# A hybrid encoder layer in float32: causal mask added on VectorE, and the feed-forward net's first gate weights in buffers of the output projection's last block

## Chip, cores and metric

The kernel runs on one core of one Trainium2 chip. The metric is the device time of one execution in microseconds (us), the median over runs. The engines are TensorE (PE, with its weight loads PEld), VectorE (DVE), ScalarE (ACT), GpSimd (POOL) and SyncE (SP), whose queue issues all DMAs here.

## Reference

One layer of a streaming encoder on x of 1024 tokens by 1024 channels, float32. Cut to what matters:

```
proj = x @ w_in                                   # q, k, v of attention; q, f, i, g of the recurrence; two gates
y_a  = fox_attention(q_a, k_a, v_a, log_f)        # 8 heads of 64: softmax(q k^T/8 + F[t] - F[s], causal) v, F = cumsum(log f)
y_b  = hgrn2(...)                                 # 4 heads of 128, gated linear recurrence, RMS norm, gate
merged = sigmoid(gate_a) * (y_a @ w_pa) + sigmoid(gate_b) * (y_b @ w_pb)
x = layer_norm(2**.25 * x + merged @ w_o, ln1_g, ln1_b)
u, g = split(x @ w_ff_in)                         # 2816 hidden channels each
x = layer_norm(2**.25 * x + (silu(g) * u) @ w_ff_out, ln2_g, ln2_b)
```

## The kernel before

**Arithmetic.** Nearly every product is three matmuls of 128x512: each operand is split into a rounded high part (a copy on ACT) and the low rest (a subtraction on DVE), and high x high, high x low and low x high are summed in PSUM (`split`, L336; `mm3`, L365). Large products go by Strassen-Winograd: seven quarter products p1 to p7 with sums of quarter operands, made on DVE (names t1 to t4, s1 to s4).

**Stages.** v projections; forget gates; the first q and k projection (`qk_first`, L624); eight attention heads in four pairs (`attention`, L667), with the next pair's q and k projection (`qk_project`); four recurrence heads (`hgrn`) with their projections; gate projections (`gate`, `GatePair`); branch projections and merge; output projection with layer norm, eight token tiles t = 0 to 7 (L1191); the feed-forward net's first product in 22 chunks of 128 hidden channels (`Chunk`, L1275; the first two chunks run together, L1352 to L1402, the others by `chunk`, L1322); its second product with the last layer norm.

**What sets the order.** Every call on an engine goes into a list (`Plan.add`, L89). `Plan.schedule` (L160) simulates the five queues with fixed costs, takes the call that could start first, and writes the calls out in that order (`issue`, L268). So each engine's order is fixed at build time, each engine works it off strictly in order, and any call that is added or moved can reorder others. All calls carry the line L279 in the profile, so instructions are told apart by the names of their tiles. Equal ready times are decided by rank; `plan.early` (L65) lowers the rank of what is built under it. Buffers come from tagged pools (L294), given in the order of first use, except for the tags in `LOOSE`; a tile waits until the one before it in its buffer is no longer used.

**Attention.** For each head the kernel loads the head's negative forget sums into two rows of `box1` by a broadcast DMA (L675), and POOL adds the causal mask to a copy for the diagonal blocks, in two halves of 128x512 (L678). DVE then adds scores and these sums and takes the maximum in one instruction (profile: CUSTOM_DVE, tiles `p<-s,box`), ACT takes the exponential with the row sum (`soft` is the small tile of maximum, sum and reciprocal), POOL divides by the row sum, and TensorE transposes (`pt`) and multiplies by the values (`pv`). In the first pair's projection TensorE's product p7 goes into the bank `qk_pt`, out of which DVE must first have read the sum u2 (`qk_u`).

**Output projection.** Its weights lie in split form, per half hf and contraction block c: c = 0, 1 in an "x" buffer (`wox`), 2, 3 in the small wh and wl buffers, 4, 5 in "kb", 6, 7 in "pf" (L1162 to L1170). A tile t takes 48 matmuls, c = 0 to 7 for hf = 0, then for hf = 1; then come residual, statistics (`lnst`), layer norm, eight transposes (`x1t`) and the splits of the net's operands (X11, X12 for t < 4, X22 and S1 to S4 for t > 3; `xs` in the profile).

**The net's entry.** The weights of chunks 0 and 1, gate and up, four blocks of 512 KB, lie in one "x" buffer (`raws`, L1353), which is the one that `wox` gives up. Products p1 and p2 of both chunks (banks `fa`, operands X11 and X12, weights `Tp1`, `Tp2`) need only gate weights and the first four token tiles; p5 and p4 (banks `fc`, `fd`) need sums with the up weights and all eight tiles.

```
    plan.early = EARLY
    raws = take("x", [4, KC, P], "w01_r")
    ks = [Chunk(c, (raws[:, 2 * c], raws[:, 2 * c + 1])) for c in range(2)]
    banks = [[next_bank(f"f{n}{c}") for n in "abcd"] for c in range(2)]
```

Of the kernel before, what the change touches and what calls it, by code (L numbers as in the profile page):

```python
# [11 lines left out]
AF = mybir.ActivationFunctionType  # L12
# [4 lines left out]
P = 128  # L17
S = 1024
D = 1024
KC = D // P  # L20
NT = S // P
HA, DH = 8, 64
HB = 4
NB = 512
# [7 lines left out]
EARLY = 3000  # L32
# [250 lines left out]
def trunk(ctx: ExitStack, tc, a: dict, out: bass.AP):  # L283
    nc = tc.nc
    plan = Plan(tc)
    sync, act, dve, pool, pe = (plan.queue(n, e) for n, e in (
        ("SP", nc.sync), ("ACT", nc.scalar), ("DVE", nc.vector), ("POOL", nc.gpsimd), ("PE", nc.tensor)))
# [17 lines left out]
    def take(tag, shape, name, dt=F32):  # L305
        return plan.tile(root, [P] + shape, dt, tag, name, BUFS[tag])
# [4 lines left out]
    def half(tag, name, dt=F32):  # L311
        return take(tag, [NB], name, dt)
# [4 lines left out]
    def keep(shape, name, dt=F32):  # L317
        return plan.tile(cst, shape, dt, "k_" + name, name, 1)
# [46 lines left out]
    def mm3(o, lh, ll, rh, rl, first, last, more={}):  # L365
        mm(o, lh, rh, start=first, stop=False, **more)
        mm(o, lh, rl, start=False, stop=False, **more)
        mm(o, ll, rh, start=False, stop=last, **more)
# [48 lines left out]
    def load(b, cs=range(4)):  # L417
        tiles, src = b
        for c in cs:
            sync.dma_start(tiles[c // 2][:, c % 2, :], src[c])  # L420
# [21 lines left out]
    for k, b, A, p, o in ((0, b11, A11, "p1", vx), (1, b21, A12, "p2", vy)):  # L442
        T = stationary4("v" + p)
        raw = rows(b)
# [130 lines left out]
    causal = const("causal", [P, 2, P], BF16, "mask")  # L575
# [91 lines left out]
    def attention(p, qk):  # L667
        q2, k2, kl = qk
        for i in range(2):
# [5 lines left out]
            sync.dma_start(box1[:, r, :], nf_d[h].partition_broadcast(P))  # L675
            for hf in range(2):
                plain, masked = (nfx[:, b0 + 4 * hf:b0 + 4 * hf + 4].rearrange("p (j c) t -> p j c t", c=2) for b0 in (0, NT))
                pool.tensor_add(masked, plain, causal[:, None].to_broadcast([P, 2, 2, P]))  # L678
            vhl = take("hl", [NT, 2, DH], f"vhl{h}", F32R)
            vsrc = va[:, :, h * DH:(h + 1) * DH]  # L680
            split(vhl[:, :, 0, :], vhl[:, :, 1, :], vsrc)
# [1 line left out]
            for qb in range(NT):  # L683
                n = (qb + 1) * P
# [35 lines left out]
                g = qb // 4  # L720
# [20 lines left out]
    raw = half("gt", "once_r")  # L741
# [305 lines left out]
    for n in range(PLAIN + 4, 2 * KC, 2):  # L1047
        k = GatePair(n)
# [33 lines left out]
    for i, src in enumerate((ya_d, yb_d)):  # L1082
        yh, yl = [], []
        for c in range(4):
            raw = raw_load(src[c], [S], f"yr{i}{c}")
# [30 lines left out]
        s_ = blk(t % 4)  # L1116
        return mh[t // 4][:, c, s_], ml[t // 4][:, c, s_]

    lnst = take("gt", [NT, 2, 6], "lnst")

    def lnrow(gname, bname):
        res = []
# [7 lines left out]
    def stats(t, hf):  # L1130
        dve.bn_stats(lnst[:, t, hf, :], z[t][:, hs(hf)])

    def layer_norm(t, gb, st=None, out=None):
        norm = small([P, 4], "norm")
        mv, ve, rstd = norm[:, :2], norm[:, 2:3], norm[:, 3:]
        dve.bn_aggr(mv, (lnst[:, t] if st is None else st).rearrange("p a b -> p (a b)"))
        dve.tensor_scalar(ve, mv[:, 1:2], LN_EPS, None, op0=ALU.add)
        pool.tensor_tensor(rstd, ve, mhalf[:, :1], op=ALU.pow)
        for hf in range(2):
            zt = z[t][:, hs(hf)]  # L1140
            dve.scalar_tensor_tensor(zt, zt, mv[:, 0:1], gb[0][hf], op0=ALU.subtract, op1=ALU.mult)
        for hf in range(2):
            zt = z[t][:, hs(hf)]
            dve.scalar_tensor_tensor(zt, zt, rstd, gb[1][hf], op0=ALU.mult, op1=ALU.add)
            if out is not None:
                sync.dma_start(out[:, hs(hf)], zt)
# [3 lines left out]
    wo = {}  # L1150
# [20 lines left out]
    OTAGS = ("s", "s", "s", "h", "h", "pv")  # L1171
    accs = [[bank(OTAGS[(2 * t + hf) % 6], f"o{hf}_{t}") for hf in range(2)] for t in range(NT)]

    def wo_mm(t, hf, c):
        lh, ll = mtok(t, c)
        mm3(accs[t][hf], lh, ll, *wo[hf, c], c == 0, c == KC - 1)

# [11 lines left out]
    for t in range(NT):  # L1191
        if t == 0:
            for c in range(KC):
                for i in range(3):
                    for hf in range(2):
                        wo_mm(i, hf, c)
        elif t > 2:
            for hf in range(2):
                for c in range(KC):
                    wo_mm(t, hf, c)  # L1200
        for hf in range(2):
            zt = z[t][:, hs(hf)]
            dve.scalar_tensor_tensor(zt, zt, ALPHA, accs[t][hf], op0=ALU.mult, op1=ALU.add)
            stats(t, hf)
        layer_norm(t, gb1)
        s_ = blk(t % 4)
        tps = []
        for g in range(2):
            tp = bank("pt", f"x1t{t}_{g}")
            for c in range(4):  # L1210
                tr(tp[:, blk(c)], z[t][:, blk(4 * g + c)], ident)
            if t < 4:
                h, l = (X11, X12)[g]
                split(h[:, :, s_], l[:, :, s_], by4(tp))
            tps.append(by4(tp))
        if t < 4:
            continue
        if t == 4:
            X22, S1 = operand("x", "x22"), operand("x", "xs1")
            r2s = [take(f"wr{i}", [2, NB], f"r2s{i}") for i in range(2)]  # L1220
        r1, r2 = (by4(x) for x in (half(("ph", "tt")[t % 2], f"r1_{t}"), r2s[t // 2 - 2][:, t % 2, :]))
        act.copy(r1, tps[0])
        split(X22[0][:, :, s_], X22[1][:, :, s_], tps[1])
        act.copy(r2, tps[1])

        def first_sums(s_=s_, r1=r1, r2=r2, t=t):
            s1 = by4(half("gt", f"s1r{t}"))
            dve.tensor_add(s1, r1, r2)
            split(S1[0][:, :, s_], S1[1][:, :, s_], s1)

        def next_sums(s_=s_, r1=r1, r2=r2):
            dve.tensor_sub(r1, f(X11[0])[:, :, s_], r1)
            dve.tensor_add(r1, r1, f(X11[1])[:, :, s_])
            dve.tensor_sub(r2, r2, r1)

        late.append((s_, r1, r2))
        if t < NT - 1:
            first_sums()
            next_sums()
# [9 lines left out]
    def next_bank(name):  # L1249
        n = turns["bank"]  # L1250
        turns["bank"] += 1
        return bank(BANKS8[n % 8], name)
# [22 lines left out]
    class Chunk:  # L1275
        def __init__(self, c, raw=None):
            self.c = c
            self.g, self.u = raw or (take("pf", [KC, P], f"w{n}{c}_r") for n in "gu")
            for i, t in enumerate((self.u, self.g)):
                sync.dma_start(t, a["w_ff"][c, i])  # L1280
            self.r = {}

        def sums(self, *names):
            g, u = self.g, self.u
# [64 lines left out]


    first_sums()
    plan.early = EARLY  # L1352
    raws = take("x", [4, KC, P], "w01_r")  # L1353
    ks = [Chunk(c, (raws[:, 2 * c], raws[:, 2 * c + 1])) for c in range(2)]
    banks = [[next_bank(f"f{n}{c}") for n in "abcd"] for c in range(2)]
    for k, o in zip(ks, banks):
        mul(k, "p1", o[0], True, True)
        k.p1 = half("ph", f"p1_{k.c}")
        act.copy(k.p1, o[0])
    for k, o in zip(ks, banks):  # L1360
        mul(k, "p2", o[0], False, True)
        k.sl = half("gt", f"sl{k.c}")
        act.activation(k.sl, o[0], AF.Silu)
    plan.early = 0
    OPS["p5"] = S1
    for k, o in zip(ks, banks):
        k.sums("1", "2")
# [69 lines left out]
    u = [half(("wh0", "wl0", "wh1", "wl1")[i], f"fu{i}") for i in range(4)]  # L1437
    ai = {"p1": 0, "p5": 1, "p6": 2, "p7": 3, "p4": 4, "p2": 5, "p3": 6}
    gb2 = lnrow("ln2_g", "ln2_b")
    lnst = take("gt", [NT, 2, 6], "lnst2")  # L1440
    XS = ("x",) * 5
    for prod in ("p1", "p5", "p6", "p4", "p7", "p2"):
        if prod == "p7":
# [2 lines left out]
        for g in range(len(GR)):  # L1446
            d, n = group(prod, ai[prod], g)
# [149 lines left out]
```

## Time and profile before

| | |
|---|---|
| Median of 3 runs | 1478.47 us (1478.4 to 1479.2) |
| Profiled execution | 1477.74 us, of which the span is 1475.8 us |
| TensorE busy | 1451.7 us, 98% of the span |
| VectorE, ScalarE, GpSimd busy | 75%, 45%, 7% |
| DMA | 172.84 MB, mean 117 GB/s |
| Mean granted TensorE clock | 0.996 of full speed |

The profile is one execution, taken by the hardware profiler. A row "PE fa <- ACT Tp_0h: 4.0, 1, 4.0" in the view of waits says that TensorE, before an instruction on tile fa, was idle 4.0 us in total, once, until ACT had written Tp_0h. A row of the timeline has start, duration, engine, line, operation, output <- inputs, shape and count, and in brackets the idle time ahead of it with what ended it; buffer numbers are left out. Windows give each engine's busy time (and number of instructions) in a stretch and the mean granted clock. A matmul's duration overlaps the next one's; what counts is the distance of starts.

### The profile page before, as it was taken

What the parts mean: (1) busy time and instruction counts of PE and PEld (TensorE: products, weight loads), DVE (VectorE), ACT (ScalarE), POOL (GpSimd) and SP (SyncE); (2) the same over time, 40 slices, a digit from 0 to 9 for tenths busy, and PEclk for the clock granted to TensorE, in tenths of its full rate; (3) what the DMA queues carried; (4) which work ended last, traced back from release to release, by engine and by line L of the source; (5) the groups of instructions that cost most, each with busy time, mean ns of one, the idle gap of its engine ahead of it and who ended that gap; (6) DMA issues with size and microseconds to landing.
All of it is one profiled execution on the core that took longest, in us unless ns stands there. A gap on an engine that the chain in (4) does not pass through costs nothing.

```text
span 1475.8 us, 19031 instructions
## 1 busy us (share of the span) xinstructions
PE 1451.7 (98%) x6807; PEld 1190.5 (81%) x6807; DVE 1109.4 (75%) x2088; ACT 669.3 (45%) x1157; POOL 97.7 (7%) x116
## 2 busy tenths in 40 slices
PE   9999999999999999999999899999999999999998
PEld 6777878888888887788888788888888888888886
DVE  7987686676797799744848897676666666798597
ACT  6536677577466465334611443332333333434430
POOL 0012142230000001000001000000000000000000
PEclk9999999999999999999999999999999999999999
DMA  7122112111111135347710304332332335976741
GB/s 263 31 87 75 48 54 79 42 51 36 58 59 50 58 122 178 134 145 242 246 47 1 114 32 143 103 94 94 96 101 103 107 107 182 350 268 218 248 159 58
DMA packets 70287, 172.84 MB, mean 117 GB/s; under 512 B 7968, under 2 KB 8864, under 8 KB 70192
## 3 DMA queue, kind: packets, MB, share of 16 engines
q1 hardware_dynamic: 70192, 171.62, 34.9%
q8 instruction: 54, 0.88, 0.3%
q14 instruction: 41, 0.34, 0.1%
HBM read 134.57 MB, written 37.03 MB: 116 GB/s over the span
## 4 chain that ended last, share of the span: by engine, by line
PE 89%; DVE 5%; DMA 2%; ACT 2%; issue 1%; POOL 0%; SPq 0%; DVEq 0%; ACTq 0%; POOLq 0%
PE p L279 14%; PE fb L279 11%; PE fc L279 8%; PE bps L279 8%; PE fa L279 8%; PE pps L279 6%; PE o L279 6%; PE gps L279 5%; PE gs L279 5%; PE vx L279 3%; PE s L279 2%; PE pv L279 2%; PE kps L279 2%; PE pt L279 2%; PE qps L279 2%; PE vy L279 1%
## 5 line engine op out<-in xcount | busy, mean ns | idle before, releaser
L279 PE MATMUL p<-dp 128*128 128x512 f32 (+1 forms) x957 | 210.0, 382 | 0.0
L279 PEld LDWEIGHTS p<-dp 128*128 128x128 f32 x957 | 175.3, 188 | 34.8
L279 PE MATMUL fc<-xs,Tp 128*128 128x512 f32 x528 | 126.9, 389 | 0.0
L279 PE MATMUL fb<-xs,Tp 128*128 128x512 f32 x528 | 126.7, 389 | 0.0
L279 PE MATMUL fa<-x,Tp 128*128 128x512 f32 x480 | 115.7, 389 | 0.5 <-DVE u L279 0.5
L279 PEld LDWEIGHTS fc<-xs,Tp 128*128 128x128 f32 x528 | 99.0, 188 | 20.7 <-ACT xs L279 0.2
L279 PEld LDWEIGHTS fb<-xs,Tp 128*128 128x128 f32 x528 | 99.1, 188 | 20.6
L279 ACT CAST Tp<-t 128x512 fp32r<-128x512 f32 x88 | 54.5, 620 | 118.1 <-PE fc L279 71.1
L279 DVE TENSOR_TENSOR Tp<-t,Tp 128x512 fp32r<-128x512 f32 x88 | 60.7, 691 | 60.3 <-ACT Tp L279 59.9
L279 PEld LDWEIGHTS fa<-x,Tp 128*128 128x128 f32 x480 | 90.0, 188 | 19.5 <-ACT p L279 0.9
L279 ACT CAST dp<-dap 128x1024 fp32r<-128x1024 f32 (+1 forms) x42 | 41.2, 982 | 99.7 <-PE p L279 43.4
L279 PE MATMUL bps<-xh,wb_l 128*128 128x512 f32 x192 | 76.5, 399 | 0.2
L279 PE MATMUL bps<-xh,wb_h 128*128 128x512 f32 x192 | 75.7, 395 | 0.4 <-ACT hbg L279 0.4
L279 PE MATMUL bps<-xl,wb_h 128*128 128x512 f32 x192 | 75.8, 395 | 0.0
L279 POOL TENSOR_TENSOR norm<-norm,mhalf 128x1 f32<-128x1 f32 x16 | 14.6, 913 | 881.2 <-DVE norm L279 881.2
L279 DVE TENSOR_TENSOR tl<-pt,th 128x512 fp32r<-128x512 f32 (+1 forms) x96 | 50.5, 552 | 18.7 <-ACT th L279 18.1
L279 DVE TENSOR_TENSOR dp<-dap,dp 128x1024 fp32r<-128x1024 f32 (+1 forms) x42 | 47.4, 1132 | 20.1 <-ACT dp L279 20.1
L279 POOL TENSOR_SCALAR p<-p,soft 128x384 f32<-128x384 f32 (+4 forms) x64 | 48.6, 767 | 164.3 <-DVE soft L279 128.6
L279 ACT ACTIVATE p<-p,soft 128x384 f32<-128x384 f32 (+4 forms) x64 | 49.5, 774 | 20.4 <-DVE soft L279 20.0
L279 PE MATMUL fb<-x,Tp 128*128 128x512 f32 x240 | 57.7, 389 | 0.0
L279 ACT CAST th<-pt 128x512 fp32r<-128x512 f32 (+1 forms) x96 | 43.0, 478 | 25.2 <-PE pt L279 23.6
L279 PE MATMUL gps<-xh,wg_h 128*128 128x512 f32 x128 | 52.2, 408 | 1.1 <-ACT wg_h L279 1.1
(511 smaller groups left out, 3490.0 us busy)
## 6 DMA issues: line engine op xcount, KB each, us to landing
dbp<-in_w_fo SPq DMA_DIRECT2D x45, 512.0 KB, 4.7
dap<-a_d SPq DMA_DIRECT2D x35, 512.0 KB, 4.8
a_d<-ar SPq DMA_DIRECT2D x42, 256.0 KB, 3.5
wu_r<-in_w_ff SPq DMA_DIRECT2D x20, 512.0 KB, 3.9
wg_r<-in_w_ff SPq DMA_DIRECT2D x20, 512.0 KB, 3.7
a_d<-as SPq DMA_DIRECT2D x33, 256.0 KB, 2.5
wg_r<-in_w_g SPq DMA_DIRECT2D x16, 512.0 KB, 4.4
sg<-gate_d SPq DMA_DIRECT2D x32, 256.0 KB, 3.7
```

The source lines that it names most:

```text
L279: getattr(q.engine, method)(*args, **kw)
```

## The change

It does two things. The causal mask is added by DVE and not by POOL. And the net's entry is laid out anew:

- The gate weights of chunks 0 and 1 go into two "pf" buffers of their own, and p1's results into a third; only the up weights go into the "x" buffer. The gates are loaded first, the ups only after p1 and p2 are written down. `plan.early` is no longer used there.
- The output projection's last tile starts with c = 6, 7 of both halves, so that it is done with the "pf" buffers first.
- Chunk 1's four banks are taken in another order (its `fa` gets the bank tag pv and not pt).
- The statistics tile `lnst` has a buffer of its own and is used by the second layer norm too; a Silu of one element at t = 1 loads ACT's table ahead.
- A later chunk loads gate before up (`Chunk.load`: names "gu").

```
-                pool.tensor_add(masked, plain, causal[:, None].to_broadcast([P, 2, 2, P]))
+                dve.tensor_add(masked, plain, causal[:, None].to_broadcast([P, 2, 2, P]))
...
-    lnst = take("gt", [NT, 2, 6], "lnst")
+    lnst = keep([P, NT, 2, 6], "lnst")
+    warm = keep([P, 1], "warm")
...
-    def wo_mm(t, hf, c):
+    def wo_mm(t, hf, c, first=0, last=KC - 1):
         lh, ll = mtok(t, c)
-        mm3(accs[t][hf], lh, ll, *wo[hf, c], c == 0, c == KC - 1)
+        mm3(accs[t][hf], lh, ll, *wo[hf, c], c == first, c == last)
...
-            for hf in range(2):
-                for c in range(KC):
-                    wo_mm(t, hf, c)
+            ahead = (6, 7) if t == NT - 1 else ()
+            cs = ahead + tuple(c for c in range(KC) if c not in ahead)
+            for hf, c in [(hf, c) for part in (cs[:len(ahead)], cs[len(ahead):]) for hf in range(2) for c in part]:
+                wo_mm(t, hf, c, cs[0], cs[-1])
...
+        if t == 1:
+            act.activation(warm, lnst[:, t, 1, :1], AF.Silu)
...
-            for i, t in enumerate((self.u, self.g)):
-                sync.dma_start(t, a["w_ff"][c, i])
             self.r = {}
+            if not raw:
+                self.load("gu")
+
+        def load(self, names):
+            for n in names:
+                sync.dma_start(getattr(self, n), a["w_ff"][self.c, "ug".index(n)])
...
-    plan.early = EARLY
-    raws = take("x", [4, KC, P], "w01_r")
-    ks = [Chunk(c, (raws[:, 2 * c], raws[:, 2 * c + 1])) for c in range(2)]
-    banks = [[next_bank(f"f{n}{c}") for n in "abcd"] for c in range(2)]
+    graws = [take("pf", [KC, P], f"wg{c}_r") for c in range(2)]
+    uraws = take("x", [2, KC, P], "wu01_r")
+    p1s = take("pf", [2, NB], "p1s")
+    ks = [Chunk(c, (graws[c], uraws[:, c])) for c in range(2)]
+    for k in ks:
+        k.load("g")
+    banks = [[next_bank(f"f{n}{c}") for n in ("abcd", "dabc")[c]] for c in range(2)]
+    banks[1] = banks[1][1:] + banks[1][:1]
...
-        k.p1 = half("ph", f"p1_{k.c}")
+        k.p1 = p1s[:, k.c]
...
-    plan.early = 0
+    for k in ks:
+        k.load("u")
...
-    lnst = take("gt", [NT, 2, 6], "lnst2")
```

The planner then writes other orders. At the first attention head, DVE's order before (Tqkp4l, Tqkp7l are low weight parts of products p4 and p7, vhl1 the second head's values, qk0_u2 the sum u2):

```order
L279 TENSOR_TENSOR wq0_r_188<-wq0_r_188,wqk_t2_190 128x512
L279 TENSOR_TENSOR vhl0_217<-va_107,vhl0_217 128x8x64
L279 TENSOR_TENSOR Tqkp4l_216<-wq0_r_188,Tqkp4h_215 128x512
L279 TENSOR_TENSOR Tqkp7l_214<-wq0_r_188,Tqkp7h_213 128x512
L279 SCALAR_TENSOR_TENSOR q2_0_0_197<-qk0_s_194,q2_0_0_197 64x512
L279 TENSOR_TENSOR vhl1_286<-va_107,vhl1_286 128x8x64
L279 SCALAR_TENSOR_TENSOR q2_0_1_198<-qk0_s_194,q2_0_1_198 64x512
L279 TENSOR_TENSOR qk0_u2_192<-qk0_pt_195,qk0_p1_191 128x512
L279 TENSOR_TENSOR qk0_u2_192<-qk0_s_196,qk0_u2_192 128x512
```

DVE's order there now (box1 <- box1, causal is a mask add; wq1 are the next pair's q weights):

```order
L279 TENSOR_TENSOR wq0_r_188<-wq0_r_188,wqk_t2_190 128x512
L279 TENSOR_TENSOR vhl0_217<-va_107,vhl0_217 128x8x64
L279 TENSOR_TENSOR box1_104<-box1_104,causal_163 128x512
L279 TENSOR_TENSOR Tqkp4l_216<-wq0_r_188,Tqkp4h_215 128x512
L279 TENSOR_TENSOR Tqkp7l_214<-wq0_r_188,Tqkp7h_213 128x512
L279 SCALAR_TENSOR_TENSOR q2_0_0_197<-qk0_s_194,q2_0_0_197 64x512
L279 TENSOR_TENSOR box1_104<-box1_104,causal_163 128x512 x2
L279 SCALAR_TENSOR_TENSOR q2_0_1_198<-qk0_s_194,q2_0_1_198 64x512
L279 TENSOR_TENSOR qk0_u2_192<-qk0_pt_195,qk0_p1_191 128x512
L279 TENSOR_TENSOR box1_104<-box1_104,causal_163 128x512
L279 TENSOR_TENSOR qk0_u2_192<-qk0_s_196,qk0_u2_192 128x512
L279 TENSOR_TENSOR vhl1_286<-va_107,vhl1_286 128x8x64
```

Three mask adds stand ahead of the first half of u2 and one between its halves; vhl1 is put behind.

SP's order of loads at the net's entry before (wu and wg are a chunk's up and gate weights, w01 the four blocks of chunks 0 and 1):

```order
L279 DMA wo1_3_r_1486<-in_w_o 128x1024
L279 DMA wu2_r_1594<-in_w_ff 128x1024
L279 DMA wg2_r_1593<-in_w_ff 128x1024
L279 DMA w01_r_1542<-in_w_ff 128x1024 x4
L279 DMA wu3_r_1616<-in_w_ff 128x1024
L279 DMA wg3_r_1615<-in_w_ff 128x1024
```

And now:

```order
L279 DMA wo1_3_r_1487<-in_w_o 128x1024
L279 DMA wg0_r_1543<-in_w_ff 128x1024
L279 DMA wg1_r_1544<-in_w_ff 128x1024
L279 DMA wu01_r_1545<-in_w_ff 128x1024 x2
L279 DMA wg2_r_1595<-in_w_ff 128x1024
L279 DMA wu2_r_1596<-in_w_ff 128x1024
L279 DMA wg3_r_1617<-in_w_ff 128x1024
L279 DMA a_d_1541<-u3_1_1586 128x512
L279 DMA wu3_r_1618<-in_w_ff 128x1024
```

The first two chunks' gate weights are the first loads, chunk 2's come behind the ups, and chunk 3's ups behind a store of chunk 1's result.

TensorE's order before, around the transposes of the last token tile (x1t7; the rows of fa0 with x11 end chunk 0's p1):

```order
L279 MATMUL fa0_1543<-x11_1503,Tp1_0h_1551 128x512 x2
L279 MATMUL fa0_1543<-x11_1503,Tp1_0l_1552 128x512
L279 MATMUL x1t7_0_1537<-ident_162,z7_1456 128x128 x4
L279 MATMUL x1t7_1_1538<-ident_162,z7_1456 128x128 x4
L279 MATMUL fa0_1543<-x12_1504,Tp2_0h_1557 128x512 x2
L279 MATMUL fa1_1547<-x11_1503,Tp1_1h_1554 128x512 x2
```

And now:

```order
L279 MATMUL fa1_1552<-x11_1504,Tp1_1l_1558 128x512
L279 MATMUL fa0_1547<-x12_1505,Tp2_0h_1559 128x512 x2
L279 MATMUL x1t7_0_1538<-ident_162,z7_1456 128x128 x4
L279 MATMUL fa0_1547<-x12_1505,Tp2_0l_1560 128x512
L279 MATMUL x1t7_1_1539<-ident_162,z7_1456 128x128 x4
L279 MATMUL fa0_1547<-x12_1505,Tp2_0h_1559 128x512 x2
```

Chunk 1's p1 (fa1 with x11) now stands ahead of the last transposes, where it stood behind them.

## Prediction

> **What bounds the kernel now.** I read the page first, then the stages in windows of 25 us, then TensorE's own waits, then the chain and the timelines at the two places where it waits. The profiled execution took 1477.74 us, of which the span is 1475.8; the three runs have a median of 1478.47, so the profile lies 0.73 below the number to be predicted. The page's head:
> ```profile
> span 1475.8 us, 19031 instructions
> PE 1451.7 (98%) x6807; PEld 1190.5 (81%) x6807; DVE 1109.4 (75%) x2088; ACT 669.3 (45%) x1157; POOL 97.7 (7%) x116
> ```
> TensorE is idle for 1475.8 - 1451.7 = 24.1 us in all. The change can win only there, or where TensorE's clock is reduced. Next the windows: span, then busy time and count of PE, PEld, DVE, ACT, POOL, then the granted clock, DMA share and rate.
> ```profile
> 100.00:125.00 25.00, 19.17 (x80) 14.77 (x79) 20.32 (x45) 15.70 (x31) 6.98 (x8) 0.93 0.20 64
> 125.00:150.00 25.00, 25.00 (x135) 20.48 (x134) 19.60 (x81) 16.09 (x37) 9.23 (x11) 1.00 0.28 91
> 825.00:850.00 25.00, 20.99 (x90) 16.49 (x89) 21.88 (x37) 14.59 (x26) 0.92 (x1) 0.93 0.45 169
> 850.00:875.00 25.00, 24.74 (x110) 20.14 (x108) 24.31 (x41) 10.71 (x19) 0.00 (x0) 1.00 0.00 1
> 900.00:925.00 25.00, 25.00 (x112) 20.71 (x111) 16.37 (x26) 7.99 (x14) 0.00 (x0) 1.00 0.42 137
> ```
> Two windows stand out. In 100:125 (first attention head) TensorE is idle 25 - 19.17 = 5.8 us, and a mean clock of 0.93 costs about 25 x 0.07 = 1.75 us more: 7.6 lost. In 825:850 (entry of the feed-forward net) it is idle 4.0 us and again loses 1.75. Elsewhere it is full, as in 125:150 and 900:925. Both lie where the change acts. TensorE's waits (us in total, times, longest) name who was late:
> ```profile
> PE fa L279 <- ACT Tp_0h L279: 4.0, 1, 4.0
> PE qk_pt L279 <- DVE qk_u L279: 3.1, 1, 3.1
> PE ot L279 <- DVE ob L279: 1.4, 2, 0.8
> PE s L279 <- DVE soft L279: 1.2, 1, 1.2
> PE gps L279 <- ACT wg_h L279: 1.1, 1, 1.1
> PE fa L279 <- DVE u L279: 0.5, 1, 0.5
> ```
>
> **Part 1, the mask on VectorE.** The POOL and DVE timelines around the first head (start, duration, instruction), and the two PE rows beside the gap:
> ```profile
> 98.55 6.31 POOL L279 TENSOR_TENSOR box<-box,causal 128x512 f32<-128x512 f32 x4 [98.11 <-DVE qk_p L279]
> 140.11 2.27 POOL L279 TENSOR_TENSOR box<-box,causal 128x512 f32<-128x512 f32 x2
> 98.43 0.68 DVE L279 TENSOR_TENSOR Tqkp6l<-wqk_t,Tqkp6h 128x512 fp32r<-128x512 f32 x1
> 99.03 1.65 DVE L279 TENSOR_TENSOR wq_r<-wq_r,wqk_t 128x512 f32<-128x512 f32 x1
> 103.76 1.65 DVE L279 TENSOR_TENSOR Tqkp7l<-wq_r,Tqkp7h 128x512 fp32r<-128x512 f32 x1
> 107.60 0.69 DVE L279 TENSOR_TENSOR qk_u<-qk_pt,qk_p 128x512 f32<-128x512 f32 x1
> 104.92 0.39 PE L279 MATMUL qk_s<-vs4h,Tqkp3l 128*128 128x512 f32 x1
> 108.43 0.47 PE L279 MATMUL qk_pt<-vs3h,Tqkp7h 128*128 128x512 f32 x1 [3.13 <-DVE qk_u L279]
> 102.16 0.33 SPq L279 DMA_DIRECT2D wq_r<-in_w_qk  x1
> wq_r<-in_w_qk SPq DMA_DIRECT2D x1, 512.0 KB, 3.7
> ```
> While POOL's four adds run (98.55 to 104.86), four DVE operations of one size take 1.65 each, the first and the last of them shown, where the row before took 0.68. POOL's adds suffer too: 6.31 / 4 = 1.58 against 2.27 / 2 = 1.14 later. So they share something and take turns, and the four DVE rows need about 103.76 + 1.58 - 99.03 = 6.3 us instead of 4 x 0.60 = 2.4. That delays the sum u2 (qk_u) by 3.9 us, and TensorE stands 3.13 us at 108.43 for it.
>
> A mask add on DVE is not in this trace. Its nearest row is any f32 operation with two SBUF inputs of 128x512:
> ```profile
> L279 DVE TENSOR_TENSOR xl<-box,xh x4: 691/692/693, 93.0 to 95.9; 128x512 fp32r<-128x512 f32 x4
> 850.22 0.69 DVE L279 TENSOR_TENSOR xs<-r,xs 128x512 fp32r<-128x512 f32 x1
> 850.82 0.69 DVE L279 TENSOR_TENSOR xs<-r2s,xs 128x512 fp32r<-128x512 f32 x1
> ```
> 0.69 each, and 0.60 from start to start in a row. No reason puts it below that or near POOL's 1.14, so I take 0.60; sixteen make 9.6 us of DVE over the attention stage. By the order, two more rows than now (three adds in, the next head's value split put behind) stand ahead of u2: 107.60 - 3.9 + 1.2 = 104.9, done at 105.5, against 105.15, when TensorE has finished its row of 104.92. Of 3.1 us about 0.4 stays: 2.7 gained. What is late next is the first head's softmax (the 1.2 us wait for soft and the 1.1 for wg_h). There the new order puts half of the next pair's q projection, 12 matmuls or 2.7 us, before those scores; its weights, issued at 102.16 and 3.7 us under way, are there at 105.9. That is as much work as the two waits. Of the remaining 7.6 - 3.1 = 4.5 us (waits and reduced clock) I take three quarters, 3.3, since the scores themselves still wait for softmax. Part 1 in this place: 2.7 + 3.3 = 6.0, bounds 3.1 (only the wait for u2) and 7.6 (all).
>
> The other twelve adds lie where TensorE is full and DVE is at 19.60 of 25 (125:150): 12 x 0.60 = 7.2 us on DVE, free as long as projections cover it. POOL's queue gets shorter, and nothing waits for it. The Trainium skill's page "Perfetto Trace Analysis" (Optimizing Scalar/DVE Operations) says that work of a saturated vector engine may be offloaded, even to GpSimd, though the shared SBUF read port may eat it up; that speaks against this part. By it the 9.6 us would be paid, and the sum would be 10.5 - 9.6 = 0.9; the window row says that VectorE isn't saturated there, and the four rows of 1.65 show the port.
>
> The order also shifts the projections between the stages: fewer gate matmuls are used up in attention, so the last gate block now lies around the last head's output transposes. That covers most of TensorE's 1.4 us at ot; I take 0.9, bounds 0 and 1.4. The idle time scattered elsewhere is about 5 us, and reordering moves it by 1.5 either way.
>
> **Part 2, the entry of the feed-forward net.** From SP's timeline, the chain, DVE and the page's DMA part:
> ```profile
> 826.10 0.33 SPq L279 DMA_DIRECT2D wu_r<-in_w_ff  x1
> 827.72 1.75 SPq L279 DMA_DIRECT2D w_r<-in_w_ff  x4
> 813.53 10.72 PE o L279 x47
> 828.10 6.98 DMA w_r<-in_w_ff
> 835.10 0.63 ACT Tp_0h L279
> 835.77 4.89 PE fa L279 x12
> wg_r<-in_w_ff SPq DMA_DIRECT2D x20, 512.0 KB, 3.7
> ```
> Chunk 2's weights are issued first, then the four of chunks 0 and 1, as soon as the output projection's buffer is free; the gate weights land at 835.1, 3.5 us after the last o matmul (831.6). Then 12 matmuls take 4.89 us instead of 12 x 10.72 / 47 = 2.74, because the clock is reduced. After the change the last block starts with rows 6 and 7. It starts at 831.6 - 48 x 0.228 - 0.9 (eight transposes in it) = 819.8; the buffers are free after 6 and 12 matmuls, 821.2 and 822.5. At 3.7 us they land at 824.9 and 826.2; chunk 0's is cast (0.63) and split (0.69) before 828, over 3 us ahead of need. The up-weights' buffer comes 6 matmuls (1.4 us) later than now, 828.9, lands at 832.6 and its second half about a us later, and DVE first reads it twelve rows behind 831.8, near 838. So the 4.0 us, the 1.75 of clock and the later 0.5 wait (DVE u) can all go: 6.2. Two details are free: chunk 1's first bank no longer waits for the last transposes, and ACT's table load leaves this stretch, where ACT isn't what TensorE waits for.
>
> But DVE is the next to be late. It is busy 24.31 of 25 in 850:875:
> ```profile
> 831.80 0.69 DVE L279 SCALAR_TENSOR_TENSOR z<-z,o 128x512 f32<-128x512 f32 x1 [0.46 <-PE o L279]
> 842.28 0.69 DVE L279 TENSOR_TENSOR x<-x1t,x 128x512 fp32r<-128x512 f32 x1 [1.44 <-ACT x L279]
> 868.52 0.69 DVE L279 TENSOR_TENSOR xs<-r2s,xs 128x512 fp32r<-128x512 f32 x1 [0.69 <-ACT xs L279]
> 877.61 5.00 PE fc L279 x22
> ```
> From the last output tile (831.80) to the last subtraction of the p3 operand, behind which the 22 fc matmuls start at 877.61, DVE works almost without a pause. In the new order this stretch has three rows fewer (chunk 0's two splits done before it, two of chunk 2's sums put behind it, one of chunk 2's splits put into it): 3 x 0.60 = 1.8. The pauses of 1.44 and 0.69 go with the earlier transposes: 2.1. It starts 0.3 late, since two splits now precede it. So DVE gets there 1.8 + 2.1 - 0.3 = 3.6 us sooner, TensorE could have been 6.2 sooner, and the rest returns as a new wait, about 2.4 us at chunk 2's second product and some 0.3 at the sum operand. I take 3.6; bounds 6.2 (DVE keeps up) and 3.6 - 1.75 = 1.9 (that wait brings a spell of reduced clock). From chunk 3 on DVE has room (16.37 of 25), so what is gained stays.
>
> Sum: 6.0 + 3.6 + 0.9 = 10.5. The profile would be 1477.74 - 10.5 = 1467.2, the median 1468.0.
>
> **A rule on the clock.** The row first: the reduced clock at 121 comes after pieces of idle time of 1.24 and 1.12, none long by itself.
> ```profile
> 119.00:120.00 1.00, 0.00 (x0) 0.00 (x1) 0.97 (x3) 1.00 (x4) 0.06 (x1) 1.00 0.00 0
> 121.00:122.00 1.00, 1.00 (x6) 1.00 (x5) 0.84 (x3) 1.00 (x2) 0.00 (x0) 0.50 0.09 16
> ```
> So a wait of 2.4 us at chunk 2 may cost clock too, which is why the bound above has it. The Trainium skill's page "TensorE: Matmul & The Clock Gate" (HAM oscillation) asks for a gap over about 3.4 us before the clock is reduced. By it that spell would not come, and the small case below would be 1473.5 - 1.75 = 1471.7; this trace shows one after shorter gaps.
>
> **The rivals.** First, everything goes: VectorE's rows are spread so that TensorE never waits. 7.6 + 6.2 + 1.4 = 15.2, 1463.3. For it: both losses have a named cause that disappears. Against: 24.31 of 25 on DVE. Second, the small case: only the wait for u2 goes, the softmax waits stay, and chunk 2's new wait reduces the clock: 3.1 + 1.9 = 5.0, 1473.5. For it: those softmax waits are not POOL's. Third, the change moves the loss and doesn't remove it: both parts win only their lower bounds, and the reordered projections meet new waits of 3.5 us, the scattered 5 us grown by two thirds: 3.1 + 1.9 - 3.5 = 1.5, 1477. Fourth, slower: the adds now stand in DVE's own queue behind a DMA.
> ```profile
> DMA to landing us min/median/max: 3.3/3.8/4.0
> ```
> That is for the broadcast of a head's forget sums (box). POOL could wait for it with nothing behind it; on DVE the softmax reductions of the running head queue behind, TensorE waits for those, and its order is fixed. If each of the six later heads' first adds stood the whole 3.8 us and TensorE felt it, that is 22.8: 1478.5 - 10.5 + 22.8 = 1490.8. It decides from 10.5 / 6 = 1.75 us per head. Against it: POOL waited for such a DMA only once, for 0.45 us, and TensorE has projections between the scores.
>
> **How the numbers follow.** Chances: the forecast 0.55 (own range 1465 to 1471), all goes 0.15, the small case 0.18, moved 0.07, slower 0.05. Less than 0.2% (3 us) can't be told from no change here. The first three are faster: 0.88; the fourth is the same: 0.07; slower: 0.05. The range 1463 to 1474 holds the first three with their bounds; what is left out is the last two and the ends.
>
> **What would show it.** Right: DVE rows near 100 us at 0.69 and the gap before qk_pt below 0.6; no wait of fa for Tp_0h, and 12 fa matmuls in 2.74; a new TensorE wait of 1 to 3 us about 35 us behind the last o matmul; window sums full elsewhere. Wrong: a clock of 0.93 still in the windows at 100 or 850; TensorE waiting for soft in several heads, with DVE idle before box for a DMA; a wait for DVE at the net's entry as long as the 4.0 that went.

## The result, and the profile after

The changed kernel takes 1465.05 us (median of 4 runs, 1464.36 to 1466.74) against 1478.84 before (1478.4 to 1480.13): a ratio of 0.9907, 95% interval 0.989 to 0.9924. The forecast was 1468.0, range 1463 to 1474. The profiled executions took 1477.74 and 1464.36 us, 13.4 apart, where the sum of the prediction was 10.5: each of its gains came, and the terms for the stages between the first head and the net were too small.

The page's head after the change:

```profile
span 1462.3 us, 19057 instructions
PE 1448.3 (99%) x6807; PEld 1189.4 (81%) x6807; DVE 1112.4 (76%) x2104; ACT 669.1 (46%) x1158; POOL 77.1 (5%) x100
```
TensorE's idle time is 1462.3 - 1448.3 = 14.0 us, 10.1 less. First three windows behind the first head, TensorE alone, in the kernel before (span, busy time and count, granted clock, DMA share, rate). The third holds the waits at ot, for which the prediction took 0.9; what else is idle here it left to "scattered" time:

```profile
200.00:225.00 25.00, 24.39 (x134) 1.00 0.10 32
225.00:350.00 125.00, 124.30 (x650) 1.00 0.20 57
550.00:650.00 100.00, 97.62 (x444) 1.00 0.41 140
```
The same three in the changed kernel:

```profile
200.00:225.00 25.00, 25.00 (x129) 1.00 0.17 52
225.00:350.00 125.00, 124.87 (x650) 1.00 0.17 50
550.00:650.00 100.00, 99.21 (x446) 1.00 0.46 149
```
Here the idle time falls from 0.61 + 0.70 + 2.38 = 3.7 to 0 + 0.13 + 0.79 = 0.9. The windows that the prediction went by, in the changed kernel (all engines, as there):

```profile
100.00:125.00 25.00, 23.59 (x110) 18.33 (x108) 22.51 (x66) 19.30 (x38) 3.06 (x6) 1.00 0.17 59
825.00:850.00 25.00, 24.90 (x113) 20.13 (x112) 25.00 (x44) 12.97 (x23) 0.92 (x1) 1.00 0.14 46
850.00:875.00 25.00, 23.11 (x101) 18.42 (x100) 24.40 (x42) 9.21 (x16) 0.00 (x0) 1.00 0.35 117
```
At 100 us idle time fell from 5.83 to 1.41, and the clock is full: 4.4 + 1.75 = 6.2 gained (forecast 6.0), and TensorE begins 110 instructions there and not 80. At 825 idle time is 0.1, VectorE is busy without a gap, and at 850 a new 1.9 of idle time stands, with a full clock. Two of TensorE's waits:

```profile
PE fa L279 <- ACT Tp L279: 1.7, 1, 1.7
PE qk_pt L279 <- DVE qk_u L279: 0.4, 1, 0.4
```
The 4.0 for Tp_0h and the 1.4 at ot are gone, the 3.1 for u2 is 0.4, and a wait of 1.7 is new. The timeline at these places:

```profile
100.91 0.68 DVE L279 TENSOR_TENSOR box<-box,causal 128x512 f32<-128x512 f32 x1
102.12 0.68 DVE L279 TENSOR_TENSOR Tqkp7l<-wq_r,Tqkp7h 128x512 fp32r<-128x512 f32 x1
106.43 0.47 PE L279 MATMUL qk_pt<-vs3h,Tqkp7h 128*128 128x512 f32 x1 [0.44 <-DVE qk_u L279]
811.57 0.80 SPq L279 DMA_DIRECT2D wg_r<-in_w_ff  x2
816.35 1.14 ACT L279 CAST Tp_0h<-wg_r 128x512 fp32r<-128x512 f32 x2
822.49 0.68 DVE L279 SCALAR_TENSOR_TENSOR z<-z,o 128x512 f32<-128x512 f32 x1
860.84 0.73 PE L279 MATMUL fa<-x,Tp 128*128 128x512 f32 x2 [1.72 <-ACT Tp L279]
```
VectorE's rows near 100 us take 0.68 and not 1.65, and a mask add there takes 0.68 too. The last output tile stands at 822.49 (before: 831.80), so 9.3 us are won ahead of the net and 13.4 - 9.3 = 4.1 at its entry. The new wait is the one that the prediction named, at chunk 2's second product.

So the windows show 6.2 at the first head and 3.7 - 0.9 = 2.8 in later attention and recurrence. They don't show all. Two TensorE rows that both kernels have, the first qk_pt matmul and the first o matmul, before:

```profile
100.61 0.39 PE L279 MATMUL qk_pt<-vs2h,Tqkp6h 128*128 128x512 f32 x1
738.00 0.62 PE L279 MATMUL o<-wox,mh 128*128 128x512 f32 x2
```
And after:

```profile
101.30 0.39 PE L279 MATMUL qk_pt<-vs2h,Tqkp6h 128*128 128x512 f32 x1
728.58 0.62 PE L279 MATMUL o<-wox,mh 128*128 128x512 f32 x2
```
The changed kernel's execution is 0.7 behind when the first head begins and 9.4 ahead at the first o matmul. So 10.1 are gained between these rows, of which the windows show 9.0, and 4.1 from there to the end of the span. The 0.7 need not be the change's: over the fourteen profiles of this case the first row stands anywhere from 100.61 to 101.86, at 100.76 in one with all adds on VectorE (e6). A difference of up to 1.3 us between two single executions is therefore better read from the distance of such rows than from the whole span.

### The profile page after: what moved, and what is told of

It reads as the page before. It is cut to its first block, busy times and chain, and to the rows that moved or that the text cites. A ratio compares the mean times of both kernels' runs of the same rounds, so it can differ in the third digit from the quotient of the medians.

```text
span 1462.3 us, 19057 instructions
## 1 busy us (share of the span) xinstructions
PE 1448.3 (99%) x6807; PEld 1189.4 (81%) x6807; DVE 1112.4 (76%) x2104; ACT 669.1 (46%) x1158; POOL 77.1 (5%) x100
## 4 chain that ended last, share of the span: by engine, by line
PE 91%; DVE 5%; DMA 1%; ACT 1%; issue 1%; SPq 0%; POOL 0%; DVEq 0%; ACTq 0%
PE p L279 14%; PE fb L279 12%; PE bps L279 8%; PE fc L279 8%; PE fa L279 7%; PE pps L279 6%; PE o L279 6%; PE gs L279 5%; PE gps L279 5%; PE vx L279 3%; PE pv L279 2%; PE kps L279 2%; PE pt L279 2%; PE qps L279 2%; PE s L279 2%; PE vy L279 1%
## 5 line engine op out<-in xcount | busy, mean ns | idle before, releaser
L279 POOL TENSOR_SCALAR p<-p,soft 128x128 f32<-128x128 f32 (+3 forms) x64 | 48.8, 769 | 267.2 <-DVE soft L279 230.4
L279 ACT ACTIVATE p<-p,soft 128x128 f32<-128x128 f32 (+3 forms) x64 | 49.6, 776 | 10.7 <-DVE soft L279 9.1
L279 ACT CAST Tp<-wg_r 128x512 fp32r<-128x512 f32 x40 | 24.9, 623 | 61.3 <-PE fb L279 31.4
```

What stands on the lines that cost most here:

```text
L279: getattr(q.engine, method)(*args, **kw)
```

## The experiments

Theory: on GpSimd the mask adds and VectorE's operations take turns and delay u2, and the new order of the projections fills the softmax waits (part 1); at the net's entry VectorE is the next limit (part 2). Main rivals: only one of the two mechanisms of part 1 acts; at the entry something other than VectorE limits. All times are medians; the kernel before, beside them, took 1479.41 (first four runs), 1478.98 (next four), 1479.70 and 1479.46.

### The two parts apart

```diff
 e1: kernel before
-                pool.tensor_add(masked, plain, ...)
+                dve.tensor_add(masked, plain, ...)
 e2: changed kernel
-                dve.tensor_add(masked, plain, ...)
+                pool.tensor_add(masked, plain, ...)
```


> The kernel before with the sixteen mask adds on VectorE; the net's entry as before. Theory (both parts act by themselves; the changed kernel was 9.4 us ahead at the first o matmul and gained 4 more behind it): 9 to 10 us faster than before, the windows at 100 us filled as in the changed kernel, the 4.0 us wait of fa for Tp_0h still there. Rival (the two parts share one gain, TensorE's order is shifted by either): 11 or more here and little in the run with the entry alone. Rival of the prediction's sizes: 6.9 (6.0 + 0.9).

> The changed kernel with the mask adds back on GpSimd. Theory: 4 us faster than before (3.5 to 4.5), with the wait for u2 of 3 us and the clock of 0.93 at 100 us still there, and a wait of 1.5 to 2.5 us at chunk 2. Rival (VectorE isn't the limit at the entry, the earlier wait there came from what the mask moved): 6 or more. Rival (the entry gains nothing by itself): under 1.

The mask alone: 1469.42, ratio 0.993 (0.9917 to 0.9942), 10.0 us faster. The entry alone: 1476.23, ratio 0.9974 (0.9965 to 0.9983), 3.2 faster. The first is what was expected; the second is a little under the expected 3.5 to 4.5, with an interval of 2.5 to 5.2. Their sum, 13.2, is about the 13.8 of both, so neither lives on the other. The mask's part is well above the prediction's 6.9. TensorE's waits with the mask alone:

```profile
PE fa L279 <- ACT Tp_0h L279: 4.3, 1, 4.3
PE qk_pt L279 <- DVE qk_u L279: 0.5, 1, 0.5
```
And with the entry alone:

```profile
PE qk_pt L279 <- DVE qk_u L279: 3.1, 1, 3.1
PE fa L279 <- ACT Tp L279: 1.7, 1, 1.7
PE ot L279 <- DVE ob L279: 1.4, 2, 0.7
```
Each removes its own waits and leaves the other's about as they were; the new 1.7 comes with the entry.

### Part 1: which engine adds, and in which order all runs

The order is worked out from each engine's assumed cost, so moving the adds changes two things at once: the engine and everybody's order. Two kernels change one each. They mark the adds, plan them for one engine and issue them on the other:

```diff
 e3: planned for GpSimd, issued on VectorE (e4: the reverse)
-                getattr(q.engine, method)(*args, **kw)
+                eng = self.queues["DVE"].engine if i in self.masks else q.engine
+                getattr(eng, method)(*args, **kw)
```


> The kernel before, its order of instructions worked out as if GpSimd added the mask, and the sixteen adds then issued on VectorE at that place. Theory (turn-taking delays u2, and the new order of the projections fills the softmax waits): the first goes and the second stays: 3 to 5 us faster, the gap before qk_pt under 0.6, waits of a us for soft and for wg_h as before. Rival (turn-taking is all of it): 8 to 9 faster. Rival (order is all of it): under 1.5.

> The kernel before, its order worked out as if VectorE added the mask, and the adds then issued on GpSimd at that place. Theory: the four VectorE rows near 100 us still take 1.65 beside GpSimd's, TensorE waits 2.5 to 4 us for u2, and only the cover of the softmax waits is gained: 2 to 5 us faster than before. Rival (order is all of it): 8 to 9 faster. Rival (turn-taking is all of it): within 1 of before.

The order kept: 1479.63, ratio 0.9998 (0.999 to 1.0006): nothing gained, where 3 to 5 were expected. The new order with GpSimd's adds: 1472.76, ratio 0.9952 (0.9939 to 0.9965), 6.65 faster, above the 2 to 5 that the theory gave it. So my half of the theory that needs only the turn-taking falls: by itself its end is worth nothing here. In the kernel with the order kept, VectorE and TensorE show why (two lines are added, so all calls carry L281):

```profile
102.78 0.69 DVE L281 TENSOR_TENSOR Tqkp7l<-wq_r,Tqkp7h 128x512 fp32r<-128x512 f32 x1
106.23 0.69 DVE L281 TENSOR_TENSOR box<-box,causal 128x512 f32<-128x512 f32 x1
106.96 0.69 DVE L281 TENSOR_TENSOR qk_u<-qk_pt,qk_p 128x512 f32<-128x512 f32 x1
107.80 0.47 PE L281 MATMUL qk_pt<-vs3h,Tqkp7h 128*128 128x512 f32 x1 [1.76 <-DVE qk_u L281]
116.83 0.35 PE L281 MATMUL s<-k,q 128*128 128x256 f32 x1 [1.26 <-DVE soft L281]
119.40 0.50 PE L281 MATMUL gps<-xh,wg_h 128*128 128x512 f32 x1 [1.13 <-ACT wg_h L281]
```
The rows of 1.65 are gone (0.69), but the fourth add stands right ahead of u2, and 1.76 of the wait stays. The waits of 1.26 and 1.13 are as long as before. At 119.40 TensorE is 0.6 ahead of before (120.00), and this execution was 0.7 behind at the first qk_pt matmul: 1.3 are gained at the first head. Yet from that matmul to the first o matmul it takes 638.2 us, and the kernel before 637.4. So the adds, put where the plan has no room for them on VectorE, cost about 2.2 us over the heads and eat the gain. In the kernel with the new order and GpSimd's adds, from the timeline,

```profile
103.23 1.65 DVE L281 TENSOR_TENSOR Tqkp4l<-wq_r,Tqkp4h 128x512 fp32r<-128x512 f32 x1
109.39 0.47 PE L281 MATMUL qk_pt<-vs3h,Tqkp7h 128*128 128x512 f32 x1 [3.05 <-DVE qk_u L281]
110.66 0.63 PE L281 MATMUL qk_pt<-vs3l,Tqkp7h 128*128 128x512 f32 x1
```
and its window behind the heads, TensorE alone:

```profile
550.00:650.00 100.00, 99.07 (x452) 1.00 0.41 136
```
The turn-taking and the wait for u2 are there in full, and a spell of reduced clock now follows it (0.63 and not 0.39 per matmul). Yet the softmax waits behind are gone, and so is the idle time of the 550 window (0.93, before 2.38). The order gives 6.65 of the 10.0; the engine gives the other 3.3 in the new order and nothing in the old. The two work together: the new order has room for VectorE's adds, and with them the one wait that it does not cover goes.

### Are VectorE's adds free?

```diff
 e5: changed kernel
-                dve.tensor_add(masked, plain, ...)
+                (dve if h < 2 else pool).tensor_add(masked, plain, ...)
 e6: changed kernel
                 dve.tensor_add(masked, plain, ...)
+                dve.tensor_add(masked, plain, ...)
```


> The changed kernel with only the first two heads' mask adds (four of sixteen) on VectorE and the other twelve on GpSimd again, the order worked out for that. Theory (the gain of the mask part lies at the first pair; later adds meet a full TensorE on either engine): within 1.5 us of the changed kernel, 1464 to 1467, the gap before qk_pt under 0.6. Rival (the order of the later heads carries the 3 us that the prediction didn't have): 3 or more slower, 1468 or above, with the waits at ot and at pv of the kernel before back.

> The changed kernel with each of the sixteen mask adds issued twice on VectorE (the second writes the same values): 9.6 us more of VectorE. Theory (later adds are covered, the first pair's four delay u2 as in the run with the order kept): the adds near u2 cost 1 to 2.5 us, the other twelve nothing: 1466 to 1468. Rival (VectorE's time is paid in attention): 8 to 10 slower, 1473 to 1475. Rival (all is covered): 1465.

Four adds on VectorE: 1464.22, ratio 0.9899 (0.9886 to 0.9913), 0.8 below the changed kernel with intervals that overlap. So the first pair carries the whole gain, together with the order of all later stages that comes with it. What the other twelve adds cost, if anything, these times don't resolve; from the first qk_pt to the first o matmul the profile takes 627.1 us, and the changed kernel's 627.3. All adds doubled: 1469.65, ratio 0.9939 (0.9926 to 0.9953), 4.6 slower, which is what neither side expected: 9.6 us of VectorE cost half of themselves. The expected delay of u2 is not among it, its wait is 0.4 as in the changed kernel. Where it went, in windows of TensorE:

```profile
125.00:200.00 75.00, 73.98 (x398) 1.00 0.19 62
225.00:350.00 125.00, 123.90 (x647) 1.00 0.18 53
550.00:650.00 100.00, 97.29 (x442) 1.00 0.45 150
```
1.0, 1.1 and 2.7 us are idle; in the changed kernel the three windows had 0.10, 0.13 and 0.79. The waits at ot are back:

```profile
PE ot L279 <- DVE ob L279: 0.8, 1, 0.8
PE ot L279 <- ACT Tgp_10h L279: 0.7, 1, 0.7
```
So "free as long as projections cover it" held for the real adds with little to spare. The Trainium skill's page "Perfetto Trace Analysis" (Optimizing Scalar/DVE Operations) allows the offload and adds that the shared read port may undo it. Both are seen here: leaving twelve of the adds on GpSimd is no worse (e5), and in the new order all sixteen on GpSimd cost 3.3 us (e4 against e1), with the rows of 1.65 beside the first four.

### Part 2: what the entry gains from

```diff
 e7: changed kernel
-            ahead = (6, 7) if t == NT - 1 else ()
+            ahead = ()
 e8: changed kernel
             dve.tensor_sub(r1, f(X11[0])[:, :, s_], r1)
-            dve.tensor_add(r1, r1, f(X11[1])[:, :, s_])
...
         dve.tensor_sub(r2, f(X12[0])[:, :, s_], r2)
-        dve.tensor_add(r2, r2, f(X12[1])[:, :, s_])
```


> The changed kernel with the last output block's rows in their old sequence 0 to 7, so that the gate weights' buffers come free only at its end. Theory (the early release is what the entry gains from): the wait of fa for Tp_0h is back with 3 to 4.5 us, and the clock with it; 3.5 to 4.5 slower than the changed kernel, 1468.5 to 1469.5. Rival (chunk 2's weights no longer go first, and that alone is the gain): under 1 slower, 1465 to 1466. Rival (part of each): 2, with a wait of 2 to 3.

> The changed kernel without the eight adds that bring the low halves into the operands S2, S3 and S4 of the net's entry (that part of the computation is left out): 4.8 us less on VectorE between the last o matmul and chunk 2. Theory (VectorE is the limit there): the new wait of 1.7 at chunk 2's second product and the 0.2 behind it go, 1.5 to 2 us faster than the changed kernel, about 1463.2. Rival (ScalarE's queue in order is the limit, its casts stand behind a Silu): the wait stays over 1.2 and the time within 0.5 of 1465.

Without the early release: 1466.45, ratio 0.9915 (0.9901 to 0.9929), 1.4 slower, and not 3.5 to 4.5. The interval overlaps the changed kernel's, but the profile agrees: from the first o matmul to the end it takes 735.6 us, the changed kernel 733.7. Its rows at the last output block and at chunk 2:

```profile
817.23 0.80 SPq L279 DMA_DIRECT2D wg_r<-in_w_ff  x2
820.94 1.15 ACT L279 CAST Tp_0h<-wg_r 128x512 fp32r<-128x512 f32 x2 [0.52 <-DMA wg_r<-in_w_ff]
861.77 0.73 PE L279 MATMUL fa<-x,Tp 128*128 128x512 f32 x2 [2.15 <-ACT Tp L279]
```
A window of 1 us behind that wait (all engines; the clock is the third number from the end):

```profile
864.00:865.00 1.00, 1.00 (x4) 0.71 (x3) 1.00 (x3) 0.00 (x0) 0.00 (x0) 0.50 0.81 315
```
The wait for Tp_0h stays away. The gate weights lie in "pf" buffers now, and half 0's two come free in the middle of the last block whatever its rows' order; the load is issued at 817.23, 5.7 us later than in the changed kernel and still in time. The last o matmul starts at 822.50 here and at 831.38 before. Counted from it, the load goes out 2.0 earlier than before (828.10 there) and is under way 3.7 and not 7.0 (to 820.94; before to 835.08). So the larger part of what removed the 4.0 is that the gates no longer queue behind chunk 2's weights and an up block, and the smaller that they no longer wait for the up weights' buffer. This is read from the traces; no run parts the two. The rows 6 and 7 serve something else: with them VectorE makes chunk 0's splits before its dense stretch (from 817.09 there, at 822.38 and 823.58 here), and without them the wait at chunk 2 is 2.15 and not 1.72, followed by a spell at half clock (0.50). This is the case behind the prediction's lower bound for the entry, seen in a run: the entry gains 737.8 - 735.6 = 2.2 there, the bound was 1.9.

With eight VectorE operations left out: 1462.44, ratio 0.9891 (0.9877 to 0.9904), 2.6 faster than the changed kernel, against the 1.5 to 2 expected. One of its four runs took 1465.61, and the intervals overlap; the profile takes 731.4 us from the first o matmul to the end, 2.3 less than the changed kernel's. The 1.72 is gone:

```profile
859.01 0.73 PE L279 MATMUL fa<-x,Tp 128*128 128x512 f32 x2 [0.37 <-ACT p L279]
```
So VectorE was the limit behind the cast that the wait names. In the changed kernel that cast stands in ScalarE's queue behind a Silu that itself waits for VectorE:

```profile
858.64 0.63 ACT L279 ACTIVATE p1s<-p1s 128x512 f32<-128x512 f32 x1 [2.36 <-DVE p1s L279]
```

### The details that the prediction called free

```diff
 e10: changed kernel; e12: the second hunk alone
-    banks = [[next_bank(f"f{n}{c}") for n in ("abcd", "dabc")[c]] for c in range(2)]
-    banks[1] = banks[1][1:] + banks[1][:1]
+    banks = [[next_bank(f"f{n}{c}") for n in "abcd"] for c in range(2)]
...
-            act.activation(warm, lnst[:, t, 1, :1], AF.Silu)
```


> The changed kernel without the rotation of chunk 1's banks and without the early Silu that loads ScalarE's table in the output projection. The prediction called both free. Theory: within 0.7 us of the changed kernel's 1465.1; the table load of about 1.3 us then stands on ScalarE near the net's first Silu, where ScalarE has slack. Rival (they are part of the 4 us of the entry): 1.5 or more slower, with TensorE waiting for sl or for a bank within 10 us of the last o matmul.

> The changed kernel without the early Silu alone; chunk 1's banks stay rotated. ScalarE's table load of 1.28 us then stands before the net's first Silu, behind both copies of p1. Theory (the rotation is what the run with both undone lacked: there the copy of chunk 1's p1, for which its bank had to wait, came after the table load): within 0.6 us of 1465.0, no wait of fa for p1s. Rival (the table load itself delays ScalarE's casts to the point where TensorE waits): 1 to 2 slower, 1466 to 1467, with a wait for Tp or xs within 12 us of the last o matmul.

Both undone: 1466.68, ratio 0.9911 (0.9896 to 0.9926), 1.7 above the changed kernel beside it; its five runs spread from 1465.02 to 1469.16 and two of them lie within the changed kernel's. The early Silu alone undone: 1463.76, ratio 0.989 (0.9869 to 0.9911), 1.2 below. So the rival has the first by its median, not clear of the spread, and the trace shows a loss that the rotation prevents. TensorE and ScalarE with both undone:

```profile
831.89 1.28 ACT L279 ACT_TABLE_LOAD   x1
833.19 0.60 ACT L279 ACTIVATE sl<-fa 128x512 f32<-128x512 f32 x1
834.14 0.60 ACT L279 COPY p1s<-fa 128x512 f32<-128x512 f32 x1
834.80 0.73 PE L279 MATMUL fa<-x,Tp_1h 128*128 128x512 f32 x2 [1.89 <-ACT p1s L279]
```
A window of 1 us behind it:

```profile
836.00:837.00 1.00, 1.00 (x4) 0.81 (x3) 0.85 (x3) 0.82 (x2) 0.00 (x0) 0.50 0.62 250
```
Chunk 1's first product stands behind the last transposes in TensorE's order, as in the kernel before, so its copy (p1s) comes late on ScalarE and stands behind the table load and the Silu of chunk 0. TensorE waits 1.89 for it, and the clock drops. With the rotation alone kept, both copies are done ahead of the table load:

```profile
827.32 0.59 ACT L279 COPY p1s<-fa 128x512 f32<-128x512 f32 x1 [1.61 <-PE fa L279]
831.63 1.28 ACT L279 ACT_TABLE_LOAD   x1
```
Whether the early Silu costs something in the changed kernel stays open: the result is outside the expected 0.6, the two intervals overlap, and the profile without it has a wait of 0.9 at chunk 2 in place of 1.7.

### A version that is faster than both

If VectorE is the limit up to chunk 2, work that nobody needs there should go behind it. This kernel adds the mask on VectorE for the first pair alone, and puts off the end of the gate product of chunks 0 and 1:

```diff
+LATE = 300
...
             u3 = ring(f"u3_{k.c}")
         dve.tensor_add(u3, o[1], k.p1)
-        dve.tensor_add(k.p1, o[3], u3)
-        act.activation(k.p1, k.p1, AF.Silu)
-        dve.tensor_add(u3, o[2], u3)
+        dve.tensor_add(k.p1, o[2], u3)
+        plan.early = -LATE
+        dve.tensor_add(u3, o[3], u3)
+        act.activation(u3, u3, AF.Silu)
         dve.tensor_mul(u3, u3, k.p1)
+        plan.early = 0
```


> The run with the first pair's mask alone on VectorE, and in the net's entry chunk 0's and 1's second gate product is finished later: the add of fd, the Silu and the multiplication stand behind chunk 2's sums, four VectorE rows (2.4 us) and two ScalarE rows less ahead of chunk 2's second product. Theory (VectorE is the limit there, as the run without the eight adds showed: 4.8 us less took away all of 1.9): the wait of 1.7 falls to 0.6 or less and 1 to 1.5 us are gained on the first-pair run: 1462.7 to 1463.3. Rival (the rows only change places and TensorE waits for the p3 operand or for a buffer instead): within 0.4 of 1464.2.

> The changed kernel as it is, on the chip of the two runs beside it: 1465 within 1 us; the yardstick for them, nothing else.

1462.35 (1461.49 to 1463.11), ratio 0.9882 (0.9869 to 0.9896), beside the changed kernel's 1465.00 (1464.45 to 1466.34), ratio 0.9902 (0.9888 to 0.9915). The ratios' intervals overlap a little, the runs of the two do not. The expectation of 1 to 1.5 below the first-pair run was met by its mechanism (0.2 of the wait is left) and a little exceeded in size (1464.22 to 1462.35 is 1.9, from two separate comparisons). Its window at chunk 2, all engines:

```profile
850.00:875.00 25.00, 24.78 (x110) 20.19 (x108) 24.86 (x42) 10.50 (x18) 0.00 (x0) 1.00 0.30 88
```
And its timeline there (calls carry L280):

```profile
857.40 0.62 ACT L280 CAST Tp<-wg_r 128x512 fp32r<-128x512 f32 x1 [1.46 <-DVE xs L280]
863.30 1.28 DVE L280 TENSOR_TENSOR u<-fd,u 128x512 f32<-128x512 f32 x2
```
The idle time of the 850 window falls from 1.9 to 0.2: the cast for chunk 2's second product is done by 858.0, and the adds of fd stand behind, at 863.30.

All profiles by the two TensorE rows shown above, one execution each:

| Run | first qk_pt to first o, us | first o to end, us |
|---|---|---|
| before | 637.4 | 737.8 |
| e1, mask alone | 627.3 | 738.1 |
| e2, entry alone | 637.7 | 734.2 |
| e3, order kept | 638.2 | 737.8 |
| e4, order new | 631.3 | 737.4 |
| changed; e11, changed again | 627.3; 627.5 | 733.7; 733.7 |
| e5, first pair | 627.1 | 733.8 |
| e6, adds twice | 632.7 | 733.8 |
| e7, no early release | 627.8 | 735.6 |
| e8, eight operations left out | 627.1 | 731.4 |
| e9, late gating | 627.1 | 731.8 |
| e10, both details undone | 628.0 | 736.1 |
| e12, early Silu undone | 627.2 | 733.0 |

Kernels that share a part agree in it within 0.9 us, so the two parts act apart, as e1 and e2 said. The differences at the entry by which e7 to e10 were judged, 1.9 to 2.4 us, are larger than that; e12's, 0.7, is not.

## Why the prediction was right, point by point

**The first head, 6.0.** Measured 6.2. The wait for u2 fell by 3.13 - 0.44 = 2.7, as worked out, and the softmax waits with the clock gave the other 3.5 (forecast 3.3). The wait for soft is 0.3 and the one for wg_h is gone. What the runs correct is the weight of the reasons. I had taken 2.7 as what VectorE's adds give by themselves. They don't: in the old order they gave nothing at the end (e3), and the new order alone gave 6.65 (e4).

**The tail and the scattered time, 0.9 and nothing.** This is the term that was too small: 2.8 measured in the windows (1.6 in the one at 550, where both waits at ot went and not 0.9 of their 1.4, and 1.2 between 200 and 350), and 10.1 where the prediction had 6.9 between the first head and the net. The sizes lie within its bounds (1.4 at ot, 1.5 either way for the rest); the step that fell short is that the order's effect on the stages behind the first head was worth only the cover of ot. The order is the larger half of the change, and I priced it at two places only.

**Twelve adds free.** No cost that the runs resolve (e5); all sixteen doubled cost 4.6 (e6): right for this size, with little reserve. The sum of 0.9, in which the 9.6 us of VectorE would be paid, did not come.

**The entry, 3.6.** Measured 4.1 with both parts, 3.2 alone (3.6 in its profile). The limit was named rightly: VectorE is busy 25.00 of 25 at 825, chunk 2's second product waits 1.72 (forecast 2.4), and taking VectorE's work away or putting it off removes the wait (e8, e9). The gates' load stands at 811.57; the forecast of 821.2, moved up by the 9.4 that the changed kernel is ahead at the first o matmul, is 811.8. But the step from the early release to the vanished 4.0 was wrong: the 4.0 goes without it (e7), and by the traces mainly because the gates' load is under way 3.7 us and not 7.0.

**Two details free.** Wrong for one, as the traces show it: the wait of 1.89 is there in e10 and not in e12, and the rotation is what differs. How much of the time it is worth (1.7 by the medians) is not clear of the spread. I had seen that the bank no longer waits, and not that the copy behind it would queue behind a table load.

**The clock at chunk 2.** The bound with a spell did not come in the changed kernel, and did with 0.43 us more of wait (e7).

**The rivals.** That adds on VectorE wait for the broadcast of box: no such wait is in the trace after. That all goes (1463.3): no, 1.7 came back at chunk 2 as VectorE's limit said; the version with that moved behind reaches 1462.35. That the softmax waits stay and chunk 2's wait brings a spell (1473.5): neither came. That the change moves the loss (1477): the wait at chunk 2 is the only large new one.

## What to carry to other kernels

Where an order is planned from costs, moving one operation is two changes, the engine and the order; test them apart before giving either the credit. When a wait names a cast on one engine, follow its queue back: here the engine that was busy without a gap was another one, and putting off four rows of its work removed the wait. In a stretch with an engine at 25 of 25 don't take details for free: look at what stands behind each in its queue.

## What the hardware showed that I had not expected

The reduced clock doesn't follow the length of the wait alone. After the wait of 1.7 at chunk 2 it stayed full in each of the five profiles that have it (the changed kernel twice, e2, e5, e6); after 1.89 (e10) and 2.15 (e7) about 3 us at half clock followed. At u2 it dropped right behind 3.05 (e4) and 3.14 (e2), and did not behind the 3.13 of the kernel before, where the spell came 12 us later, behind 1.24 and 1.12. The Trainium skill's page "TensorE: Matmul & The Clock Gate" (HAM oscillation) asks for no gaps over about 3.4 us; the spells behind 1.89 and 2.15 don't agree with that as a safe limit. The same page of the Trainium skill (What's actually happening) says that the observation window runs free of the program, which would fit that 3.13 and 3.14 ended differently; no run here shows where the window lay.

GpSimd's adds and VectorE's rows with two SBUF inputs advance nearly in step, about 1.58 us each, when both run (e4, as before), where VectorE needs 0.60 a row by itself. Four adds beside four rows so take 6.3 us, and all eight on VectorE, at the 0.60 that e3 shows for both kinds, 8 x 0.60 = 4.8: for such adds a second engine made the pair slower than one.
